# Attention's scores and values cut into more and narrower matmuls in a two-layer hybrid trunk

## Chip, cores and metric

The kernel runs on one core of one Trainium2 chip. The metric is the device time of one execution in microseconds (us); the time before is the median of three runs.

## What is computed

The reference runs two layers over 256 tokens of 2048 channels. Each layer has a convolution branch and an attention branch that read one input projection, are gated, merged and projected out. What matters here is the attention: 16 heads, queries and keys of 128 + 64 (rotary) elements, values of 128, and a mask by chunks of 64 tokens.

```python
def chunk_causal_attention(q, k, v):
    ...
        s = jnp.einsum('bqhd,bkhd->bhqk', q_i, k,
                       preferred_element_type=jnp.float32) * scale
        q_chunk = (i * Q_BLOCK + jnp.arange(Q_BLOCK)) // CHUNK
        mask = key_chunk[None, :] <= q_chunk[:, None]
        s = jnp.where(mask, s, -jnp.inf)
        p = jax.nn.softmax(s, axis=-1).astype(v.dtype)
        return jnp.einsum('bhqk,bkhd->bqhd', p, v)
    ...
    o = lax.map(block, (qb, jnp.arange(nb)))
```

Two query blocks of 128 tokens are swept. The first sees 128 keys, the second 256.

## The kernel before

**Precision.** Matmul operands are float32r. Each float32 operand is split into a high part (a copy to float32r) and a low part (the rest); a product is the sum of high x high, low x high and high x low, three matmuls into one PSUM accumulator.

**The big products.** All weights stream from HBM in 680 pieces (`raw`) of two k-tiles. ScalarE writes the high part `hi` of a piece (`split_hi`, line 211), VectorE the low part `lo` (`split_lo`, line 220), and TensorE multiplies (`product`, lines 325 to 360) into the `acc` tiles, twelve matmuls a piece, 512 columns each for most. A piece is one *slot*. The tokens are two tiles, `t` = 0 and 1.

**What sets the order.** Every engine's instructions are issued in program order (`InOrder`, lines 127 to 144; line 135 is where all of them are recorded, so all rows of the profile say L135). Between two pieces `background` (line 252) lets due steps run: `at_slot(ahead, f, vec, act)` files a step for a slot with its cost in microseconds on VectorE and ScalarE, and what those engines have left over in a slot is filled with taps of the convolution (`fill`, `run_fill`, line 281; `tap`, line 972; `assist` lets ScalarE scale a tap ahead). So a smaller cost for a step moves taps earlier.

**Attention.** It runs in pairs of heads, 8 pairs a layer, as steps between the pieces (`attention`, line 763; slots at the head of the file). For a pair, `qk_t` holds the transposed operands: `nope_t[:, 0]` and `[:, 1]` are the high and low parts of q, `[:, 2]` and `[:, 3]` those of k; `rope_t[:, 0]` is the rotary part of q (high part in one half of the partitions, low part in the other), `rope_t[:, 1]` that of k (its high part in both halves), `rope_l` the low part of k with zeros in the other half. `rope_k` is a view of `rope_t[:, 1]` and `rope_l` together.

- `scores` (line 835): the first query tile goes to `s0`, of two halves of 128 columns a head. One matmul streams two runs of 128 key columns side by side (high and low parts of k), so the halves have to be added afterwards: three matmuls a head, of 256, 128 and 256 columns. The second query tile goes to `s1`: five matmuls a head of 256 columns, straight into one accumulator.
- `maxima` (line 859): ScalarE copies one half of `s0` into `sx` in SBUF, VectorE adds the other half, masks, and takes the negated maxima of `sx` and `s1`.
- `exponentials` (line 873) on ScalarE, then the probabilities are turned and split into `pt`, high and low.
- `values` (line 899): into `o_ps`, again two halves a head: matmuls of 512, 128, 256 and 256 columns. `outputs` (line 911): ScalarE copies one half into `o_sb`, VectorE adds the other.

In the trace the PSUM tiles of the scores are named `s`, the buffers of `pt` and of the values `pv`.

Of the kernel before, what the change touches and what calls it, by code (L numbers as in the profile page):

```python
# [11 lines left out]
F32 = mybir.dt.float32  # L12
# [3 lines left out]
ALU = mybir.AluOpType  # L16
AX = mybir.AxisListType
PSUM = bass.MemoryType.PSUM

P = 128  # L20
T = 2
SEQ = 256
# [17 lines left out]
CHUNK = 64  # L40
EPS = 1e-6
MASKED = -3.0e38
# [26 lines left out]
STATS_AT, SCALE_AT, QK_BACK_AT, QK_TURN_AT, NOPE_AT, ROPE_AT, SCORES_AT = 2, 4, 7, 11, 12, 14, 17  # L69
EXP_AT, P_BACK_AT, P_TURN_AT, P_SPLIT_AT, VALUES_AT, O_AT = 19, 23, 28, 29, 32, 34  # L70
# [53 lines left out]
def trunk(ctx: ExitStack, tc: tile.TileContext, xT, x, g_in, pos, win, wuq, wukv, wpc, wpm, wo, cst, rows, invf, out):  # L124
# [19 lines left out]
    pe, vec, act, gps, sp = (InOrder(e) for e in (nc.tensor, nc.vector, nc.scalar, nc.gpsimd, nc.sync))  # L144
# [7 lines left out]
    work = pool("work", 1)  # L152
# [7 lines left out]
    tp_p = pool("tp", 1, space=PSUM)  # L160
    s_p = pool("s", 1, space=PSUM)
# [68 lines left out]
    steps, clock, late, early = [], [0], [], []  # L230
    fill, budget, marks, owed, assist = deque(), {"vec": 0.0, "act": 0.0}, {}, [], []

    def at_slot(ahead, f, vec=0.0, act=0.0, first=False):
        steps.insert(0 if first else len(steps), (clock[0] + ahead, (vec, act), f))
# [328 lines left out]
    for l in range(DEPTH):  # L563
# [84 lines left out]
        A = SimpleNamespace(pairs={}, rotary={})  # L648

        def attention_tiles(A=A, l=l):  # L650
            qk_t = big.tile([P, 16 * SEQ], F32R, tag="big", name=f"qk_t{l}")
            A.nope_t = qk_t[:, : 8 * SEQ].rearrange("p (i h s) -> p i h s", i=4, h=2)
            A.rope_t = qk_t[:, 8 * SEQ : 12 * SEQ].rearrange("p (i h s) -> p i h s", i=2, h=2)
            A.rope_k = qk_t[:, 10 * SEQ : 14 * SEQ].rearrange("p (i h s) -> p i h s", i=2, h=2)
            A.rope_l = qk_t[:, 12 * SEQ : 14 * SEQ].rearrange("p (h s) -> p h s", h=2)
            gps.memset(A.rope_l.bitcast(F32), 0.0)
            pv = big.tile([P, 4096], F32R, tag="big", name=f"pv{l}")
            A.pt = pv[:, : 2 * 768].rearrange("p (i h q) -> p i h q", i=2, h=2)
            v_parts = [pv[:, 1536 + i * 512 : 2048 + i * 512] for i in range(5)] + [qk_t[:, 14 * SEQ :]]
            v_parts = [a.rearrange("p (t h d) -> p t h d", t=T, h=2) for a in v_parts]  # L660
            A.v_split = [v_parts[2 * j : 2 * j + 2] for j in range(3)]
            A.o_sb = big.tile([P, N_HEADS, SEQ], F32, tag="big", name=f"o_sb{l}")
            A.rinv = layer_c.tile([P, T, N_HEADS], F32, tag="rinv", name="rinv")

        def pair_of(b, A=A):
            if b not in A.pairs:


                A.pairs[b] = dict(
                    qk=work2.tile([P, T, 4, 6, 32], F32, tag="qk", name="qk"),  # L670
                    vh=A.v_split[b % 3][0],
                    vl=A.v_split[b % 3][1],
                    ss=small.tile([P, 2, T, 2], F32, tag="ss_p", name="ss_p"),
                )
            return A.pairs[b]
# [86 lines left out]

        def attention(b, pair_of=pair_of, ss_d=ss_d, kpe=kpe, ccq=ccq, ssq_t=ssq_t, gqk=gqk, A=A):
            p, st = pair_of(b), {}
            nope_t, rope_t, rope_k, rope_l = A.nope_t, A.rope_t, A.rope_k, A.rope_l
            qk, ss = p["qk"], p["ss"]

            def stats():
# [64 lines left out]
                at_slot(1, lambda: [vec.tensor_sub(lo, z, hi.bitcast(F32)) for lo, z, hi in subs], 1.8)  # L833

            def scores():
                s0 = s_p.tile([P, 2, 2, P], F32, tag="s0", name="s0")
                s1 = s_p.tile([P, 2, SEQ], F32, tag="s1", name="s1")

                for h in range(2):
                    qs = slice(0, P)  # L840
                    pe.matmul(s0[:, h], rope_t[:, 0, h, qs], rope_k[:, :, h, qs], start=True, stop=False)
                    pe.matmul(s0[:, h, 0, :], nope_t[:, 1, h, qs], nope_t[:, 2, h, qs], start=False, stop=False)
                    pe.matmul(s0[:, h], nope_t[:, 0, h, qs], nope_t[:, 2:4, h, qs], start=False, stop=True)
                for h in range(2):
                    qs = slice(P, SEQ)
                    terms = [
                        (rope_t[:, 0, h, qs], rope_t[:, 1, h, :]),
                        (nope_t[:, 0, h, qs], nope_t[:, 2, h, :]),
                        (nope_t[:, 0, h, qs], nope_t[:, 3, h, :]),
                        (nope_t[:, 1, h, qs], nope_t[:, 2, h, :]),  # L850
                        (rope_t[:, 0, h, qs], rope_l[:, h, :]),
                    ]
                    for n, (qa, ka) in enumerate(terms):
                        pe.matmul(s1[:, h, :], qa, ka, start=n == 0, stop=n == len(terms) - 1)
                st["s"] = s0, s1

                late.append(maxima)

            def maxima():
                s0, s1 = st["s"]  # L860
                sx = work.tile([P, 2, P], F32, tag="sx", name="sx")
                act.copy(sx, s0[:, :, 1, :])
                vec.tensor_add(sx, s0[:, :, 0, :], sx)
                for s, nkeys in ((sx, P), (s1, SEQ)):

                    vec.memset(s[:CHUNK, :, nkeys - CHUNK :], MASKED)
                nb = small.tile([P, T, 2], F32, tag="nb", name="nb")
                vec.tensor_reduce(nb[:, 0], sx, axis=AX.X, op=ALU.max, negate=True)
                vec.tensor_reduce(nb[:, 1], s1, axis=AX.X, op=ALU.max, negate=True)
                vec.tensor_mul(nb, nb, st["rs"])  # L870
                st["s"], st["nb"] = (sx, s1), nb

            def exponentials():

# [24 lines left out]
            def values():  # L899


                st["o"] = tp_p.tile([P, 2, 2, SEQ], F32, tag="tp", name="o_ps")
                pt, v = A.pt, (p["vh"], p["vl"])
                for h in range(2):
                    o = st["o"][:, h]
                    pe.matmul(o, v[0][:, 0, h, :], pt[:, :, h, :SEQ], start=True, stop=False)
                    pe.matmul(o[:, 0, P:], v[1][:, 1, h, :], pt[:, 0, h, SEQ:], start=False, stop=False)
                    pe.matmul(o[:, :, P:], v[0][:, 1, h, :], pt[:, :, h, SEQ:], start=False, stop=False)
                    pe.matmul(o[:, 0, :], v[1][:, 0, h, :], pt[:, 0, h, :SEQ], start=False, stop=True)

            def outputs():
                o = A.o_sb[:, 2 * b : 2 * b + 2, :]
                act.copy(o, st["o"][:, :, 0, :])
                late.append(lambda: vec.tensor_add(o, st["o"][:, :, 1, :], o))
                A.pairs.pop(b)

            def later(ahead, *args, **kw):
                at_slot(ahead + PAIR_LATER[b], *args, **kw)
# [4 lines left out]
            later(QK_TURN_AT, blockwise, 1.85)  # L923
            later(NOPE_AT, split_nope, 0.0, 1.8)
            later(ROPE_AT, split_rope, 0.0, 2.5)
            later(SCORES_AT, scores, 1.85, 0.35)
            later(EXP_AT, exponentials, 0.0, 3.3)
            later(P_BACK_AT, lambda: back_in("p"))
            later(P_TURN_AT, turn_p, 0.9)
            later(P_SPLIT_AT, split_p, 0.0, 0.8)  # L930
            later(VALUES_AT, values)
            later(O_AT, outputs, 0.62, 0.6)


        us, vs, keep = {}, {}, {"separated": {}}
        s1 = layer_c.tile([P, 2, SEQ], F32, tag="s1c", name="s1c")
# [339 lines left out]
        for kind, i, pl in planned:  # L1276
            if kind == "glu":
                at = EVAC_AT
                if i == 0 and l == 0:
                    at = 6  # L1280
# [18 lines left out]
            elif kind == "uq":  # L1299
                if i == 0:  # L1300
                    attention_tiles()
# [3 lines left out]
                if block == 2:  # L1305
                    at_slot(EVAC_AT + LAST_ROTATE_AT, lambda b=GROUP * group + 3: rotate_q(b), 1.3)
                    attention(GROUP * group + 2)
# [137 lines left out]
```

## Time and profile before

| what | value |
|---|---|
| time, median of three runs | 1876.65 us (1876.35 to 1876.85) |
| span of the profiled execution, first to last instruction | 1875.0 us |
| granted TensorE clock, mean | 1.000 |
| TensorE busy, matmuls | 1869.4 us, 8577 matmuls |
| VectorE busy | 1578.0 us |
| ScalarE busy | 1360.5 us |
| GpSimd busy | 495.7 us |
| rows of matmuls into `s` / `o_ps` | 256 / 128 |

The page gives the profiled execution's span and no other time for it; the median of the runs is 1.65 us longer. In the rows, an instruction is named by line, engine, operation and out<-in tiles, then a count. PE is a matmul, PEld its weight load (LDWEIGHTS), which overlaps matmuls. Matmuls overlap each other in the pipeline, so the sum of their durations is more than the time they take; the spacing of their starts is what counts. In the list of waits a row gives who waited for whom, the sum in us, how often, and the longest. In the list of groups, the columns are count | busy us, mean ns of one | idle us before them and what ended it.

### The profile page before, as it was taken

To read this page: it belongs to the slowest core of one execution; us is meant where nothing else is said; L and a number is where in the kernel's file an instruction comes from. 1 tells how busy PE (TensorE), PEld (TensorE's weight loads), DVE (VectorE), ACT (ScalarE), POOL (GpSimd) and SP (SyncE) were. 2 spreads that over 40 slices of the span, in tenths; PEclk is the share of its full clock that TensorE was granted. 3 is DMA by queue.
4 is the path that set the end of the run, shared out by engine and by line. 5 is a ranking of instruction groups with operands and counts; after the bars stand their busy time and mean duration, and the time that the engine had idled before them with its cause. 6 is when DMAs were issued, how large, how long until landed. Compare 5 with 4: busy or idle time off the path is not lost.

```text
span 1875.0 us, 27166 instructions
## 1 busy us (share of the span) xinstructions
PE 1869.4 (100%) x8577; PEld 1570.9 (84%) x8577; DVE 1578.0 (84%) x2453; ACT 1360.5 (73%) x2510; POOL 495.7 (26%) x942
## 2 busy tenths in 40 slices
PE   9999999999999999999999999999999999999999
PEld 8988888888888888888899888888888888888887
DVE  6899998898999988766679899889899999885664
ACT  7678888888888876644557688788889888574442
POOL 1055555542200000122221455555322000001210
PEclk9999999999999999999999999999999999999999
DMA  9688878787765566678876787887877556667775
GB/s 322 219 264 255 261 256 258 257 275 226 244 204 192 194 207 218 208 239 278 290 234 216 260 267 253 260 255 262 267 231 242 196 191 204 206 206 222 239 250 166
DMA packets 138960, 445.05 MB, mean 237 GB/s; under 512 B 23680, under 2 KB 29312, under 8 KB 138816
## 3 DMA queue, kind: packets, MB, share of 16 engines
q1 hardware_dynamic: 105120, 359.89, 59.2%
q0 software_dynamic: 32832, 82.62, 13.8%
q8 instruction: 67, 1.10, 0.2%
q10 hardware_dynamic: 864, 0.80, 0.1%
q14 instruction: 77, 0.63, 0.1%
HBM read 399.18 MB, written 44.04 MB: 236 GB/s over the span
## 4 chain that ended last, share of the span: by engine, by line
PE 99%; DMA 1%; DVE 0%; ACT 0%; SPq 0%; issue 0%; DVEq 0%
PE acc L135 96%; PE s L135 2%; PE o_ps L135 1%; DMA raw<-in_win 0%; DMA gx<-in_g 0%; DVE xres L135 0%; ACT hi L135 0%; PE var L135 0%; PE mu L135 0%; SPq L135 0%; DVEq L135 0%
## 5 line engine op out<-in xcount | busy, mean ns | idle before, releaser
L135 ACT CAST hi<-raw 128x1024 fp32r<-128x1024 f32 (+3 forms) x682 | 700.3, 1033 | 405.0 <-PE acc L135 348.9
L135 DVE TENSOR_TENSOR lo<-raw,hi 128x1024 fp32r<-128x1024 f32 (+3 forms) x682 | 814.0, 1195 | 191.5 <-PE acc L135 145.7
L135 PE MATMUL acc<-hi,hT 128*128 128x512 f32 (+2 forms) x1728 | 419.6, 382 | 0.0
L135 PEld LDWEIGHTS acc<-hi,hT 128*128 128x128 f32 x1728 | 319.6, 188 | 59.1
L135 PE MATMUL acc<-hi,h_hi 128*128 128x512 f32 (+2 forms) x864 | 260.5, 383 | 1.3 <-ACT hi L135 1.3
L135 PE MATMUL acc<-hi,h_lo 128*128 128x512 f32 (+2 forms) x864 | 260.1, 382 | 0.0
L135 ACT ACTIVATE tap<-u_t,cst 128x256 f32<-128x256 f32 x542 | 235.7, 501 | 2.8 <-DVE v_t L135 2.8
L135 PE MATMUL acc<-lo,h_hi 128*128 128x512 f32 (+2 forms) x864 | 229.7, 382 | 0.0
L135 PE MATMUL acc<-lo,hT 128*128 128x512 f32 (+2 forms) x864 | 229.3, 382 | 0.0
L135 DVE TENSOR_TENSOR v_t<-v_t,tap 128x512 f32<-128x512 f32 x271 | 186.4, 688 | 9.7 <-DVE v_t L135 0.9
L135 POOL DMA_DIRECT2D turned<-turn_d x88 | 49.4, 562 | 531.0 <-DVE v_t L135 315.0
L135 PEld LDWEIGHTS acc<-hi,h_lo 128*128 128x128 f32 x864 | 161.0, 188 | 30.1
L135 PEld LDWEIGHTS acc<-hi,h_hi 128*128 128x128 f32 x864 | 160.0, 188 | 30.9 <-ACT hi L135 2.2
L135 PEld LDWEIGHTS acc<-lo,h_hi 128*128 128x128 f32 x864 | 160.5, 188 | 30.2 <-DVE lo L135 0.3
L135 PEld LDWEIGHTS acc<-lo,hT 128*128 128x128 f32 x864 | 160.6, 188 | 29.9
L135 DVE SCALAR_TENSOR_TENSOR v_t<-u_t,cst,v_t 128x256 f32<-128x256 f32 x418 | 178.4, 480 | 2.0
L135 POOL DMA_DIRECT2D turn_d<-gate x184 | 100.5, 554 | 290.6 <-DVE gate L135 177.6
L135 PE MATMUL acc<-hi,ycT 128*128 128x512 f32 x512 | 127.8, 389 | 0.0
L135 PE MATMUL acc<-hi,oT 128*128 128x512 f32 x512 | 127.7, 389 | 0.0
L135 PE MATMUL acc<-hi,yT 128*128 128x512 f32 x512 | 127.5, 388 | 0.0
L135 PE MATMUL acc<-hi,qkc 128*128 128x512 f32 x448 | 115.4, 389 | 0.0
L135 PEld LDWEIGHTS acc<-hi,ycT 128*128 128x128 f32 x512 | 96.1, 188 | 20.0
(176 smaller groups left out, 2227.1 us busy)
## 6 DMA issues: line engine op xcount, KB each, us to landing
raw<-in_win SPq DMA_DIRECT2D x382, 512.0 KB, 4.2
raw<-in_wpm SPq DMA_DIRECT2D x64, 512.0 KB, 3.3
raw<-in_wpc SPq DMA_DIRECT2D x64, 512.0 KB, 4.2
raw<-in_wo SPq DMA_DIRECT2D x64, 512.0 KB, 4.9
raw<-in_wukv SPq DMA_DIRECT2D x32, 512.0 KB, 4.1
turned<-turn_d POOLq DMA_DIRECT2D x56, 256.0 KB, 4.7
raw<-in_win SPq DMA_DIRECT2D x32, 384.0 KB, 4.6
raw<-in_wuq SPq DMA_DIRECT2D x24, 512.0 KB, 4.3
```

The source lines that it names most:

```text
L135: ins = getattr(self.engine, name)(*a, **k)
```

## The change

For the first query tile `scores` now issues the same five products a head as for the second, each over one run of 128 key columns and all into one accumulator `s0` of 128 columns a head. `maxima` masks and reduces both PSUM tiles directly; `sx`, its copy and its addition go, and the exponentials read `s0` in PSUM. `values` issues six products a head, three of 256 columns (first key tile) and three of 128 (second key tile, seen by the second query tile alone), all into one accumulator; `outputs` is one copy. The planner's costs of the two steps are lowered: scores from 1.85 and 0.35 us to 1.4 and 0.0 (VectorE, ScalarE), outputs from 0.62 to 0.0 on VectorE.

```diff
@@ attention_tiles
-            A.rope_k = qk_t[:, 10 * SEQ : 14 * SEQ].rearrange("p (i h s) -> p i h s", i=2, h=2)
@@ scores
-                s0 = s_p.tile([P, 2, 2, P], F32, tag="s0", name="s0")
-                s1 = s_p.tile([P, 2, SEQ], F32, tag="s1", name="s1")
-
-                for h in range(2):
-                    qs = slice(0, P)
-                    pe.matmul(s0[:, h], rope_t[:, 0, h, qs], rope_k[:, :, h, qs], start=True, stop=False)
-                    pe.matmul(s0[:, h, 0, :], nope_t[:, 1, h, qs], nope_t[:, 2, h, qs], start=False, stop=False)
-                    pe.matmul(s0[:, h], nope_t[:, 0, h, qs], nope_t[:, 2:4, h, qs], start=False, stop=True)
-                for h in range(2):
-                    qs = slice(P, SEQ)
-                    terms = [
...
-                    for n, (qa, ka) in enumerate(terms):
-                        pe.matmul(s1[:, h, :], qa, ka, start=n == 0, stop=n == len(terms) - 1)
-                st["s"] = s0, s1
+                st["s"] = tuple(s_p.tile([P, 2, (t + 1) * P], F32, tag=f"s{t}", name=f"s{t}") for t in range(T))
+
+                for t, s in enumerate(st["s"]):
+                    qs, keys = slice(t * P, (t + 1) * P), slice(0, (t + 1) * P)
+                    for h in range(2):
+                        terms = [
+                            (rope_t[:, 0, h, qs], rope_t[:, 1, h, keys]),
+                            (nope_t[:, 0, h, qs], nope_t[:, 2, h, keys]),
+                            (nope_t[:, 0, h, qs], nope_t[:, 3, h, keys]),
+                            (nope_t[:, 1, h, qs], nope_t[:, 2, h, keys]),
+                            (rope_t[:, 0, h, qs], rope_l[:, h, keys]),
+                        ]
+                        for n, (qa, ka) in enumerate(terms):
+                            pe.matmul(s[:, h, :], qa, ka, start=n == 0, stop=n == len(terms) - 1)
@@ maxima
-                s0, s1 = st["s"]
-                sx = work.tile([P, 2, P], F32, tag="sx", name="sx")
-                act.copy(sx, s0[:, :, 1, :])
-                vec.tensor_add(sx, s0[:, :, 0, :], sx)
-                for s, nkeys in ((sx, P), (s1, SEQ)):
-
-                    vec.memset(s[:CHUNK, :, nkeys - CHUNK :], MASKED)
                 nb = small.tile([P, T, 2], F32, tag="nb", name="nb")
-                vec.tensor_reduce(nb[:, 0], sx, axis=AX.X, op=ALU.max, negate=True)
-                vec.tensor_reduce(nb[:, 1], s1, axis=AX.X, op=ALU.max, negate=True)
+                for t, s in enumerate(st["s"]):
+                    vec.memset(s[:CHUNK, :, (t + 1) * P - CHUNK :], MASKED)
+                    vec.tensor_reduce(nb[:, t], s, axis=AX.X, op=ALU.max, negate=True)
                 vec.tensor_mul(nb, nb, st["rs"])
@@ values
-                st["o"] = tp_p.tile([P, 2, 2, SEQ], F32, tag="tp", name="o_ps")
+                st["o"] = tp_p.tile([P, 2, SEQ], F32, tag="tp", name="o_ps")
                 pt, v = A.pt, (p["vh"], p["vl"])
                 for h in range(2):
-                    o = st["o"][:, h]
-                    pe.matmul(o, v[0][:, 0, h, :], pt[:, :, h, :SEQ], start=True, stop=False)
-                    pe.matmul(o[:, 0, P:], v[1][:, 1, h, :], pt[:, 0, h, SEQ:], start=False, stop=False)
-                    pe.matmul(o[:, :, P:], v[0][:, 1, h, :], pt[:, :, h, SEQ:], start=False, stop=False)
-                    pe.matmul(o[:, 0, :], v[1][:, 0, h, :], pt[:, 0, h, :SEQ], start=False, stop=True)
+                    for t, own, at in ((0, slice(0, SEQ), slice(0, SEQ)), (1, slice(P, SEQ), slice(SEQ, SEQ + P))):
+                        for vi, pi in ((0, 0), (0, 1), (1, 0)):
+                            pe.matmul(
+                                st["o"][:, h, own], v[vi][:, t, h, :], pt[:, pi, h, at],
+                                start=(t, vi, pi) == (0, 0, 0), stop=(t, vi, pi) == (1, 1, 0),
+                            )
@@ outputs
-                o = A.o_sb[:, 2 * b : 2 * b + 2, :]
-                act.copy(o, st["o"][:, :, 0, :])
-                late.append(lambda: vec.tensor_add(o, st["o"][:, :, 1, :], o))
+                act.copy(A.o_sb[:, 2 * b : 2 * b + 2, :], st["o"])
@@
-            later(SCORES_AT, scores, 1.85, 0.35)
+            later(SCORES_AT, scores, 1.4, 0.0)
-            later(O_AT, outputs, 0.62, 0.6)
+            later(O_AT, outputs, 0.0, 0.6)
```

In the built order TensorE's rows change only inside these groups. At the first pair's scores of the first layer, between matmuls of the running big product (`acc`), as one piece of the difference (`s_2073` is `s0`, `s_2074` is `s1`):

```order
 L135 MATMUL acc_0_1909<-lo_1990,h_hi 128x512 x2
 L135 MATMUL acc_1_1910<-lo_1990,h_hi 128x512 x2
-L135 MATMUL s_2073<-qk_t_1397 128x256
-L135 MATMUL s_2073<-qk_t_1397 128x128
-L135 MATMUL s_2073<-qk_t_1397 128x256 x2
-L135 MATMUL s_2073<-qk_t_1397 128x128
-L135 MATMUL s_2073<-qk_t_1397 128x256
+L135 MATMUL s_2073<-qk_t_1397 128x128 x10
 L135 MATMUL s_2074<-qk_t_1397 128x256 x10
 L135 MATMUL acc_0_1909<-hi_1992,h_hi 128x512 x2
```

Six matmuls into `s0` become ten of 128 columns; the ten into `s1` and the neighbours stay.

TensorE at the first pair's values, before:

```order
L135 MATMUL acc_1_2311<-lo_2499,h_hi 128x512 x2
L135 MATMUL o_ps<-pv_1399 128x512
L135 MATMUL o_ps<-pv_1399 128x128
L135 MATMUL o_ps<-pv_1399 128x2x128
L135 MATMUL o_ps<-pv_1399 128x256
L135 MATMUL o_ps<-pv_1399 128x512
L135 MATMUL o_ps<-pv_1399 128x128
L135 MATMUL o_ps<-pv_1399 128x2x128
L135 MATMUL o_ps<-pv_1399 128x256
L135 MATMUL acc_0_2593<-hi_2501,qkc_155 128x512 x4
```

and now:

```order
L135 MATMUL acc_1_2312<-lo_2506,h_hi 128x512 x2
L135 MATMUL o_ps<-pv_1399 128x256 x3
L135 MATMUL o_ps<-pv_1399 128x128 x3
L135 MATMUL o_ps<-pv_1399 128x256 x3
L135 MATMUL o_ps<-pv_1399 128x128 x3
L135 MATMUL acc_0_2603<-hi_2508,qkc_155 128x512 x4
```

Eight matmuls have become twelve, in the same place.

VectorE after the first pair's scores (`maxima`, then low parts of weights and taps `v_t`), before:

```order
L135 TENSOR_TENSOR sx<-s_2073,sx 128x256
L135 MEMSET sx 64x2x64
L135 MEMSET s_2074 64x2x64
L135 TENSOR_REDUCE nb<-sx 128x2
L135 TENSOR_REDUCE nb<-s_2074 128x2
L135 TENSOR_TENSOR nb<-nb,r_p 128x4
L135 TENSOR_TENSOR lo_2102<-raw_1915,hi_2057 128x1024
L135 SCALAR_TENSOR_TENSOR v_t<-u_t,cst,v_t 128x256 x2
L135 TENSOR_TENSOR lo_2130<-raw_1951,hi_2104 128x1024
```

and now:

```order
L135 MEMSET s_2073 64x2x64
L135 TENSOR_REDUCE nb<-s_2073 128x2
L135 MEMSET s_2074 64x2x64
L135 TENSOR_REDUCE nb<-s_2074 128x2
L135 TENSOR_TENSOR nb<-nb,r_p 128x4
L135 TENSOR_TENSOR lo_2103<-raw_1915,hi_2057 128x1024
L135 SCALAR_TENSOR_TENSOR v_t<-u_t,cst,v_t 128x256 x4
L135 TENSOR_TENSOR lo_2133<-raw_1951,hi_2105 128x1024
```

The addition is gone, and two instructions of a tap that stood later have moved up ahead of the next low part. The orders of SyncE and GpSimd, which issue the DMAs, are the same as before.

More of the change, by code (lines that the diff above doesn't have):

```diff
@@ L764, in attention @@
             p, st = pair_of(b), {}
-            nope_t, rope_t, rope_k, rope_l = A.nope_t, A.rope_t, A.rope_k, A.rope_l
+            nope_t, rope_t, rope_l = A.nope_t, A.rope_t, A.rope_l
             qk, ss = p["qk"], p["ss"]
@@ L844, in scores @@
-                for h in range(2):
-                    qs = slice(P, SEQ)
-                    terms = [
[L847 to L852, printed above, removed]
-                    for n, (qa, ka) in enumerate(terms):
-                        pe.matmul(s1[:, h, :], qa, ka, start=n == 0, stop=n == len(terms) - 1)
@@ L869, in maxima @@
-                vec.tensor_reduce(nb[:, 1], s1, axis=AX.X, op=ALU.max, negate=True)
+                for t, s in enumerate(st["s"]):
+                    vec.memset(s[:CHUNK, :, (t + 1) * P - CHUNK :], MASKED)
+                    vec.tensor_reduce(nb[:, t], s, axis=AX.X, op=ALU.max, negate=True)
                 vec.tensor_mul(nb, nb, st["rs"])
-                st["s"], st["nb"] = (sx, s1), nb
+                st["nb"] = nb
             def exponentials():
```

## The prediction

> **What bounds the kernel now.** I read the page first: the busy shares and the chain of work that ended last.
>
> ```profile
> span 1875.0 us, 27166 instructions
> ...
> PE 1869.4 (100%) x8577; PEld 1570.9 (84%) x8577; DVE 1578.0 (84%) x2453; ACT 1360.5 (73%) x2510; POOL 495.7 (26%) x942
> ...
> PEclk9999999999999999999999999999999999999999
> ...
> PE 99%; DMA 1%; DVE 0%; ACT 0%; SPq 0%; issue 0%; DVEq 0%
> PE acc L135 96%; PE s L135 2%; PE o_ps L135 1%; DMA raw<-in_win 0%; DMA gx<-in_g 0%; DVE xres L135 0%; ACT hi L135 0%; PE var L135 0%; PE mu L135 0%; SPq L135 0%; DVEq L135 0%
> ```
>
> The chain is TensorE for 99%, and what the change rewrites stands on it: `s` (scores) 2%, `o_ps` (values) 1%. The granted clock is 0.9 or more in every slice. A busy TensorE is not proof of one that never waits, since ends of matmuls are modelled; so I asked next for the waits of the matmul and weight-load rows, and then for the longest pieces of the chain in order of time (start, length, what).
>
> ```profile
> PE acc L135 <- ACT hi L135: 1.3, 2, 0.9
> PE warm L135 <- PEq L1434: 0.8, 1, 0.8
> ...
> PEld acc L135 <- ACT hi L135: 2.2, 3, 1.4
> PEld warm L135 <- issue: 0.8, 1, 0.8
> PEld acc L135 <- DVE lo L135: 0.3, 1, 0.3
> ```
>
> ```profile
> 12.19 164.67 PE acc L135 x804
> 178.74 32.67 PE acc L135 x144
> ...
> 294.11 24.50 PE acc L135 x108
> 329.84 24.50 PE acc L135 x108
> ```
>
> All that TensorE waited is 1.3 + 0.8 us before matmuls and 2.2 + 0.8 + 0.3 us before weight loads, and the pieces of the chain show it running without a break from 12.19 us on. The second piece gives a price: 144 matmuls of 512 columns in 32.67 us are 0.227 us each, from start to start. The two engines that feed it are ahead of it, as the list of waits of all engines says:
>
> ```profile
> ACT hi L135 <- PE acc L135: 348.9, 277, 2.6
> DVE lo L135 <- PE acc L135: 145.7, 112, 1.8
> ```
>
> ScalarE's high parts and VectorE's low parts of the weights wait for matmuls to give their buffers back, not the other way round. So the time is a sum of matmul spacings plus the start and the tail, and only what changes that sum counts.
>
> **TensorE's part of the change.** The columns streamed do not change. Scores of the first query tile before, per head: 256 + 128 + 256 = 640; after: five products of 128 = 640. Values before, per head: 512 + 128 + 256 + 256 = 1152; after: 3 x 256 + 3 x 128 = 1152. What changes is into how many matmuls they are cut: 6 become 10 in the scores, 8 become 12 in the values, and each brings a weight load of its own. So the price of a 128-column matmul decides. The durations of the rows do not give it, since they overlap; starts do. TensorE's timeline over one pair's scores (start, length from the first start to the last end, count), then the same list from narrower windows, where a row that groups matmuls begins with the first still open:
>
> ```profile
> 176.69 2.05 PE L135 MATMUL s<-qk_t 128*128 128x256 f32 x16
> 178.58 0.40 PE L135 MATMUL acc<-hi,h_hi 128*128 128x512 f32 x1
> ...
> 177.38 0.40 PE L135 MATMUL s<-qk_t 128*128 128x256 f32 x2
> ...
> 176.81 0.40 PE L135 MATMUL s<-qk_t 128*128 128x128 f32 x2
> ...
> 176.87 0.45 PE L135 MATMUL s<-qk_t 128*128 128x256 f32 x2
> ```
>
> The sixteen matmuls take 178.58 - 176.69 = 1.89 us. The last ten, of 256 columns, run from 177.38 to 178.58: **0.120 us** each. The first six, four of 256 columns and two of 128, take 0.69 us; less 4 x 0.120 that leaves 0.21, or 0.105 us for one of 128. But the recorded starts put only 176.87 - 176.81 = 0.06 us between a 128-column matmul and the next one. The weight-load rows at the same place settle how I read that:
>
> ```profile
> 176.81 0.19 PEld L135 LDWEIGHTS s<-qk_t 128*128 128x128 f32 x1
> ...
> 176.92 0.19 PEld L135 LDWEIGHTS s<-qk_t 128*128 128x128 f32 x1
> ...
> 177.04 0.19 PEld L135 LDWEIGHTS s<-qk_t 128*128 128x128 f32 x1
> ```
>
> Loads begin 0.11 and 0.12 us apart even across the 128-column matmul: a load holds its place for about 0.11 us, the short matmul ends in half of that, and the next one, though recorded as begun, waits for its weights. The values give the same price a second time:
>
> ```profile
> 221.32 1.32 PE L135 MATMUL o_ps<-pv 128*128 128x512 f32 x8
> 222.47 0.39 PE L135 MATMUL acc<-hi,qkc 128*128 128x512 f32 x1
> ```
>
> Eight matmuls in 222.47 - 221.32 = 1.15 us: two of 512 columns (2 x 0.227), four of 256 (4 x 0.120), and 0.216 left for two of 128, 0.108 each. Bounds for a row of ten of them, which no trace shows: from below 0.105 (the scores), from above 0.120, the spacing of ten loads in a row where each carries 256 columns. Further down lies only the recorded 0.06, a rival. I take **0.108**, the weight-load gap and the values agreeing on it.
>
> - Scores of a pair: 10 x 0.108 + 10 x 0.120 = 2.28 us, before 1.89: +0.39.
> - Values of a pair: 6 x 0.120 + 6 x 0.108 = 1.37 us, before 1.15: +0.22.
> - Pairs: 8 a layer, two layers, 16. 16 x 0.61 = **+9.7 us**. With 0.105 it is 16 x (0.36 + 0.20) = +9.0, with 0.120 it is 16 x (0.51 + 0.29) = +12.8.
>
> That the halves are no longer strided side by side I price at nothing: with strided products priced like the others (0.120 in the scores, 0.227 in the values) the two groups leave 0.105 and 0.108 for a short matmul, so a stride can hardly cost more than that difference.
>
> **What VectorE and ScalarE are relieved of.** The groups of their instructions, by form:
>
> ```profile
> L135 DVE TENSOR_TENSOR o_sb<-o_ps,o_sb 128x512 f32<-128x512 f32 x16 | 11.0, 687 | 2.7 <-ACT o_sb L135 2.7
> L135 DVE TENSOR_REDUCE nb<-s 128x2 f32<-128x512 f32 x16 | 10.7, 667 | 0.0
> L135 DVE TENSOR_TENSOR sx<-s,sx 128x256 f32<-128x256 f32 x16 | 6.8, 425 | 27.4 <-ACT sx L135 27.4
> L135 DVE TENSOR_REDUCE nb<-sx 128x2 f32<-128x256 f32 x16 | 5.6, 353 | 0.0
> ...
> L135 ACT COPY sx<-s 128x256 f32<-128x256 f32 x16 | 6.0, 373 | 18.3 <-PE s L135 18.3
> ```
>
> Per pair VectorE loses the two additions, 0.687 + 0.425 = 1.11 us, and ScalarE the copy of 0.373 us. Reading the first tile's scores out of PSUM in place of `sx` I take as free: the maximum over 512 PSUM elements costs 0.667, twice the 0.353 over 256 in SBUF within 6%. All of it, 17.8 us on VectorE and 6.0 us on ScalarE, and the 27.4 us for which VectorE stood waiting for the copy, lies beside a TensorE that waits for neither: worth 0 to the end. The planner is told of it, 0.45 + 0.62 = 1.07 us a pair less for VectorE and 0.35 for ScalarE, and spends it on convolution taps, so they stand earlier, not that the engine idles. SyncE's and GpSimd's orders do not change, nor does any DMA. No wait is added: `s0` is now held until the exponentials have read it, as `s1` was already, and the next pair's scores come 329.84 - 294.11 = 35.7 us later (the last two pieces of the chain above, each between a pair's values and the next pair's scores).
>
> **Sum.** The profiled span is 1875.0 us, 1.65 below the median 1876.65 of the runs; I add the change to both. Span 1884.7, time 1876.65 + 9.7 = **1886.4 us**. What a measurement of this kernel can tell from no change is about 0.2%, 3.8 us: it ends at 1872.9 and 1880.4.
>
> **Rivals.**
>
> 1. *The recorded 0.06 is the true spacing* of short matmuls in a row, the load being drawn far enough ahead. Then scores cost 0.60 + 1.20 - 1.89 = -0.09, values 0.72 + 0.36 - 1.15 = -0.07 a pair, 16 x -0.16 = -2.6: 1874.1, not slower than before. Place: the ten 128-column matmuls of each pair. It decides from 10p + 1.20 - 1.89 + 0.72 + 6p - 1.15 = 0, a spacing p of 0.070. For it speaks the matmul rows' starts; against it that both groups then come out 0.09 to 0.10 us longer than their parts. Chance 4%.
> 2. *Loads overlap one another in a long row of short matmuls.* A load's row is 0.19 long while loads begin 0.11 apart, so there is overlap already, and ten alike might halve the gap between 0.06 and 0.108: p = 0.084 gives 16 x (0.15 + 0.07) = +3.6, 1880.2. Against it: the one gap between loads that a short matmul spans is 0.11, not less. Chance 5%. [...]
> 3. *Load and matmul take turns* where there is nothing long to hide the load: p = 0.108 + 0.06 = 0.168, scores +0.99, values +0.58, 16 x 1.57 = +25.1: 1901.8. Against it: the 0.21 and 0.216 us left for two short matmuls hold one load each and no more. Chance 4%. [...]
> 4. *TensorE begins to wait for a low part.* The planner puts earlier taps between VectorE's subtractions; two instructions more ahead of a `lo` (row below) delay it by 2 x 0.480 = 0.96 us.
>
> ```profile
> L135 DVE SCALAR_TENSOR_TENSOR v_t<-u_t,cst,v_t 128x256 f32<-128x256 f32 x418 | 178.4, 480 | 2.0
> ```
>
>    Queued behind it on VectorE are the next `lo` and the evacuations. Once in each pair would be 16 x 0.96 = 15.4 on top, 1901.8; two or three times is 1888 to 1889. Against it: VectorE is given as many microseconds as it is told to fill, and it waited 145.7 us for TensorE where TensorE waited 0.3 for it. Chance 7%.
>
> That the change does not do what it says can be left out: the built order shows the ten short matmuls a pair.
>
> **How the numbers follow.** Forecast 80%, rivals 4, 5, 4 and 7%. The forecast by its bounds is 1876.65 + 9.0 = 1885.7 to 1876.65 + 12.8 = 1889.5. The range is **1884.9 to 1890.5**: the forecast's, with 0.8 us below for rounding in rows read to 0.01 us, and 1.0 above for the mild form of rival 4. It leaves out rivals 1, 2, 3 and part of 4. Faster by over 0.2%: 0.01, the rest of rival 1 lying within the bound. Within 0.2%: 0.08 (rivals 1 and 2). Slower: 0.91.
>
> **What would show it.** In the profile after: 320 rows of score matmuls (16 x 20, where 16 x 16 = 256 stood) and 192 of the values (16 x 12); from the start of a pair's first score matmul to the next `acc` 2.28 us, of the values 1.37; weight loads 0.11 apart in the run of ten. 2.88 and 1.73 would be rival 3's turns, 1.80 and 1.08 rival 1. A row of TensorE waiting for `lo` of more than a microsecond would be rival 4, and gaps between `acc` matmuls with it. A granted clock below 1 in any slice, or spacings other than 0.227 for 512 columns, would take the ground from under the sum.

## The result, and the profile after

The changed kernel takes **1886.24 us** (five runs, 1885.83 to 1887.04) against 1876.65 (five, 1875.73 to 1876.85): a ratio of 1.0053, 95% interval 1.0041 to 1.0066. It is slower by 9.6 us, where 9.7 were forecast. The span of its profiled execution went from 1875.0 to 1884.3 us, 9.3 more.

The page after, in the lines that answer to those of before: busy times, clock, and the chain.

```profile
span 1884.3 us, 27334 instructions
...
PE 1880.1 (100%) x8705; PEld 1583.1 (84%) x8705; DVE 1570.7 (83%) x2436; ACT 1341.8 (71%) x2464; POOL 494.1 (26%) x942
...
PEclk9999999999999999999999999999999999999999
...
PE 100%; DVE 0%; issue 0%; DVEq 0%
```

128 matmuls and 128 weight loads have come (8577 to 8705; 320 rows into `s` and 192 into `o_ps`). VectorE and ScalarE are busy for 7.3 and 18.7 us less, not for the 17.8 and 6.0 us that the change takes off them. ScalarE's further 13.0 us are 30 scalings of taps that it no longer does (its row before and after, below). VectorE does these taps alone now: 448 rows of `v_t<-u_t,cst,v_t` where 418 stood, for 15 additions of scaled taps fewer. That is a part of why its busy time fell by less.

```profile
L135 ACT ACTIVATE tap<-u_t,cst 128x256 f32<-128x256 f32 x542 | 235.7, 501 | 2.8 <-DVE v_t L135 2.8
```

```profile
L135 ACT ACTIVATE tap<-u_t,cst 128x256 f32<-128x256 f32 x512 | 222.7, 499 | 3.2 <-DVE v_t L135 2.8
```

The chain is still TensorE alone. Did TensorE wait for anything new? Its waits, matmuls and then loads, and the two large waits of its feeders:

```profile
PE warm L135 <- PEq L1420: 0.8, 1, 0.8
```

```profile
PEld warm L135 <- issue: 0.8, 1, 0.8
PEld acc L135 <- ACT hi L135: 0.6, 2, 0.3
```

```profile
ACT hi L135 <- PE acc L135: 394.7, 293, 4.4
...
DVE lo L135 <- PE acc L135: 160.3, 123, 1.8
```

No. The feeders are further ahead than before (394.7 us of waiting against 348.9, 160.3 against 145.7). The time is in the matmuls that were re-cut. TensorE's timeline over the first pair's scores and over its values:

```profile
176.04 2.46 PE L135 MATMUL s<-qk_t 128*128 128x128 f32 x20
178.34 0.40 PE L135 MATMUL acc<-hi,h_hi 128*128 128x512 f32 x1
...
221.49 1.49 PE L135 MATMUL o_ps<-pv 128*128 128x256 f32 x12
222.82 0.44 PE L135 MATMUL acc<-hi,qkc 128*128 128x512 f32 x1
...
222.82 0.68 PE L135 MATMUL acc<-hi,qkc 128*128 128x512 f32 x2
```

The scores take 178.34 - 176.04 = 2.30 us (1.89 before, 2.28 forecast), the values 222.82 - 221.49 = 1.33 (1.15 before). The values seem 0.04 cheaper than the 1.37 forecast, but the 0.44 behind the last row gives them away: I read it as the `acc` matmul recorded at 222.82 waiting for a load that the short matmul ahead could not hide, since one of 512 columns lasts 0.39 otherwise. A pair's whole cost is best read from the chain, from the end of one pair's values to the end of the next one's:

```profile
295.70 24.55 PE acc L135 x108
332.06 24.55 PE acc L135 x108
```

36.36 us from pair to pair where 329.84 - 294.11 = 35.73 stood: +0.63 a pair, and 16 x 0.63 = 10.1. The span grew by 9.3, 0.8 less, and 0.65 of that lies ahead of any changed matmul: the first scores start at 176.04 in this execution and at 176.69 in the one before. The waits for the first weights differ (1.3 us before matmuls in the profile before, none after). It looks like scatter between executions: in the profiles of the experiments below the first scores start at 175.57 in `half_weights` and at 176.31 in `wide_scores`.

Inside the run of ten, the weight loads from narrow windows of the timeline, each row beginning with the first load still open:

```profile
176.04 0.30 PEld L135 LDWEIGHTS s<-qk_t 128*128 128x128 f32 x2
...
176.15 0.30 PEld L135 LDWEIGHTS s<-qk_t 128*128 128x128 f32 x2
...
176.26 0.30 PEld L135 LDWEIGHTS s<-qk_t 128*128 128x128 f32 x2
...
176.37 0.30 PEld L135 LDWEIGHTS s<-qk_t 128*128 128x128 f32 x2
```

They start 0.11 us apart, one after the other, as the single short matmuls of before had suggested.

### The profile page after: what moved, and what is told of

It reads as the page before. It is cut to its first block, busy times and chain, and to the rows that moved or that the text cites. A ratio compares the mean times of both kernels' runs of the same rounds, so it can differ in the third digit from the quotient of the medians.

```text
span 1884.3 us, 27334 instructions
## 1 busy us (share of the span) xinstructions
PE 1880.1 (100%) x8705; PEld 1583.1 (84%) x8705; DVE 1570.7 (83%) x2436; ACT 1341.8 (71%) x2464; POOL 494.1 (26%) x942
## 3 DMA queue, kind: packets, MB, share of 16 engines
q8 instruction: 68, 1.11, 0.2%
## 4 chain that ended last, share of the span: by engine, by line
PE 100%; DVE 0%; issue 0%; DVEq 0%
PE acc L135 96%; PE s L135 2%; PE o_ps L135 1%; PE warm L135 0%; DVE xres L135 0%; PE var L135 0%; PE mu L135 0%; DVEq L135 0%
## 5 line engine op out<-in xcount | busy, mean ns | idle before, releaser
L135 ACT CAST hi<-raw 128x1024 fp32r<-128x1024 f32 (+3 forms) x682 | 699.9, 1032 | 459.5 <-PE acc L135 394.7
L135 DVE TENSOR_TENSOR lo<-raw,hi 128x1024 fp32r<-128x1024 f32 (+3 forms) x682 | 813.9, 1195 | 219.1 <-PE acc L135 160.3
L135 ACT ACTIVATE tap<-u_t,cst 128x256 f32<-128x256 f32 x512 | 222.7, 499 | 3.2 <-DVE v_t L135 2.8
L135 DVE SCALAR_TENSOR_TENSOR v_t<-u_t,cst,v_t 128x256 f32<-128x256 f32 x448 | 191.1, 478 | 2.1
L135 DVE TENSOR_TENSOR v_t<-v_t,tap 128x512 f32<-128x512 f32 x256 | 175.8, 687 | 8.2
```

The source lines that it names most:

```text
L135: ins = getattr(self.engine, name)(*a, **k)
```

## The experiments

The theory: a matmul of 128 columns is held to about 0.11 us by the load of the next 128 weight columns, so the change costs TensorE 0.63 us a pair, and nothing that it gives VectorE and ScalarE reaches the end. Rivals: replanned taps make TensorE wait; narrow products stream slowly, or wait for one another in the accumulator; every added matmul costs a fixed share. Each experiment has its own runs of the kernel before on the same chip (medians of 1875.8 to 1876.3 us). The edits are shown in part, with `...` where lines are left out.

### One half of the change at a time

`scores_only` takes the changed `scores` and `maxima` and puts back the values:

```diff
...
-                st["o"] = tp_p.tile([P, 2, SEQ], F32, tag="tp", name="o_ps")
+                st["o"] = tp_p.tile([P, 2, 2, SEQ], F32, tag="tp", name="o_ps")
...
-            later(O_AT, outputs, 0.0, 0.6)
+            later(O_AT, outputs, 0.62, 0.6)
```

> The changed scores and maxima, with the values and outputs of before. Theory (a 128-column matmul is held to 0.11 us by the weight load behind it): the scores' part of the sum alone, 16 x 0.39 to 0.41 = 6.2 to 6.6 us over before, 1882.9 to 1883.3. Rival (the loss is a wait of the feeding engines, caused by the replanned taps): no fixed share; near 1876.7 or near 1886.2, with TensorE rows that wait.

Measured 1882.84 us, ratio 1.0036 (1.0023 to 1.0048), +6.8 over its own before of 1876.07. `values_only` is the reverse, the changed `values` and `outputs` in the kernel before.

> The changed values and outputs, with the scores and maxima of before. Theory: 16 x 0.22 = 3.5 us over before, 1880.2; together with scores_only the two add up to the whole change. Rival (replanned taps): the two do not add up.

Measured 1879.26, ratio 1.0017 (1.0008 to 1.0025), +3.2. The two add up to 10.0, the change measured 9.6. The chain's pieces agree; first `scores_only`, then `values_only`:

```profile
331.36 24.50 PE acc L135 x108
367.51 24.50 PE acc L135 x108
```

```profile
330.11 24.55 PE acc L135 x108
366.06 24.55 PE acc L135 x108
```

36.15 and 35.95 from pair to pair, +0.42 and +0.22 over 35.73. A loss from replanned taps would have no reason to split like that, and in neither profile does TensorE wait for more than 1.4 us for any one feeder.

### The relief alone

```diff
...
-                act.copy(sx, s0[:, :, 1, :])
-                vec.tensor_add(sx, s0[:, :, 0, :], sx)
+                sx = s0[:, :, 0, :]
...
-                late.append(lambda: vec.tensor_add(o, st["o"][:, :, 1, :], o))
+            later(SCORES_AT, scores, 1.4, 0.0)
+            later(O_AT, outputs, 0.0, 0.6)
```

> TensorE's matmuls of before, but the second halves of the first tile's scores and of the values are left out of the sums: no copy into sx, no addition of it, one copy of the values without the addition, and the planner's costs of the change. Theory: VectorE's 17.8 us and ScalarE's 6.0 us lie beside TensorE, 1876.65 within 0.7. Rival (they hold TensorE up somewhere): up to 17 us faster; a gain of 2 us or more would show it, and the change's own loss would then be larger than it looks.

Measured 1876.12 against 1876.07, ratio 1.0 (0.9991 to 1.0009). VectorE and ScalarE are as busy as in the changed kernel (1571.1 and 1341.2 us, there 1570.7 and 1341.8), so the whole relief is in it. What the change takes off the two engines is worth nothing to the end of this kernel.

### More short matmuls

`second_tile_cut` also cuts the second query tile's scores:

```diff
-                            pe.matmul(s[:, h, :], qa, ka, start=n == 0, stop=n == len(terms) - 1)
+                            for c in range(t + 1):
+                                own = slice(c * P, (c + 1) * P)
+                                pe.matmul(
+                                    s[:, h, own], qa, ka[:, own],
+                                    start=n == 0 and c == 0, stop=n == len(terms) - 1 and c == t,
+                                )
```

> The changed kernel with the second query tile's scores cut too, 20 matmuls of 128 columns a pair in place of 10 of 256; the same columns. Theory: 20 x 0.111 - 10 x 0.120 = 1.02 us a pair, 16.3 us over the changed kernel, 1902.5. Rival (a fixed cost for every added matmul, 9.6 us / 128 = 0.075): 160 x 0.075 = 12.0 over it, 1898.2. Rival (loads hidden better in a longer run): less than 10 over it.

Measured 1903.07, ratio 1.0143 (1.0128 to 1.0159) to before, 16.8 over the changed kernel: the theory's 16.3, not the 12.0 of a fixed cost. Its timeline at the first pair's scores:

```profile
176.07 3.46 PE L135 MATMUL s<-qk_t 128*128 128x128 f32 x30
179.37 0.44 PE L135 MATMUL acc<-hi,h_hi 128*128 128x512 f32 x1
```

Thirty short matmuls in 3.30 us: 0.110 each, over a run three times as long.

### Load or stream: half the columns, half the weights

Both rivals left give 0.11 for a 128-column product too: slow streaming, and waits in the accumulator. `half_columns` halves the stream and keeps the loads. To leave half the keys out it masks them for all 128 queries of the first tile; the reference masks them for the first 64 alone:

```diff
-                    qs, keys = slice(t * P, (t + 1) * P), slice(0, (t + 1) * P)
+                    qs, keys = slice(t * P, (t + 1) * P), slice(0, SEQ if t else CHUNK)
...
-                    vec.memset(s[:CHUNK, :, (t + 1) * P - CHUNK :], MASKED)
+                    vec.memset(s[: CHUNK if t else P, :, (t + 1) * P - CHUNK :], MASKED)
```

> The changed kernel, but the first query tile's scores are taken for the first 64 keys alone (the other 64 are masked for every query): ten matmuls of 64 columns a pair in place of ten of 128, with the same weight loads. Theory (the load of 128 weight columns sets the spacing): the spacing in the run stays at 0.11 and the time at 1886.2 within 0.7. Rival (a narrow product streams at about half speed, 0.11 for 128 columns): spacing about 0.055, 16 x 10 x 0.055 = 8.8 less, 1877.4.

`half_weights` halves the loads and keeps the stream:

```diff
-                    qs, keys = slice(t * P, (t + 1) * P), slice(0, (t + 1) * P)
+                    qs, keys = slice(t * P, SEQ if t else CHUNK), slice(0, (t + 1) * P)
...
```

> The changed kernel, but the first query tile's scores are taken for the first 64 queries alone (the others are set to zero): ten weight loads of 64 columns a pair in place of 128, with the same 128 columns streamed. Theory: the load halves to about 0.055 and 128 columns at full rate remain, about 0.067; 16 x 10 x 0.044 = 7.0 less than the changed kernel, 1879.2. Rival (narrow products stream slowly, or wait for one another in the same accumulator): spacing stays at 0.11, 1886.2.

The scores of a pair in `half_columns`, then in `half_weights` (the columns name weights, rows by columns, and the product's output):

```profile
175.85 2.46 PE L135 MATMUL s<-qk_t 128*128 128x64 f32 x20
178.15 0.40 PE L135 MATMUL acc<-hi,h_hi 128*128 128x512 f32 x1
```

```profile
175.57 2.01 PE L135 MATMUL s<-qk_t 128*64 128x128 f32 x20
177.41 0.40 PE L135 MATMUL acc<-hi,h_hi 128*128 128x512 f32 x1
```

Half the columns change nothing: 2.30 us, and 1886.12 against the changed kernel's 1886.24. Half the weights give 1.84 us, 0.46 less over ten matmuls, so about 0.065 each, and 1878.93, 7.3 us less where 7.0 were expected (7.2 less than `half_columns`, which ran on the same chip). The loads follow, 0.11 apart in the first and 0.06 in the second:

```profile
175.97 0.30 PEld L135 LDWEIGHTS s<-qk_t 128*128 128x128 f32 x2
176.08 0.30 PEld L135 LDWEIGHTS s<-qk_t 128*128 128x128 f32 x2
```

```profile
175.57 0.20 PEld L135 LDWEIGHTS s<-qk_t 128*64 128x64 f32 x2
175.63 0.19 PEld L135 LDWEIGHTS s<-qk_t 128*64 128x64 f32 x2
```

The same 128 columns into the same accumulator, one behind the other, run at 0.065 when the load is short. That settles it for the load, with one reserve: the rows of the output are halved with the columns of the weights, and no run parts the two. The load of 128 columns shows as 0.11 us between loads; what one of 64 takes alone no run shows, since 128 columns are streamed behind each and the spacing is 0.065.

### The opposite edit

If narrow costs, wide should save a little. `second_tile_wide` goes back to the kernel before and lays the second tile's scores side by side as well:

```diff
...
-                        pe.matmul(s1[:, h, :], qa, ka, start=n == 0, stop=n == len(terms) - 1)
+                    pe.matmul(s1[:, h], rope_t[:, 0, h, qs], rope_k[:, :, h, :], start=True, stop=False)
+                    pe.matmul(s1[:, h, 0, :], nope_t[:, 1, h, qs], nope_t[:, 2, h, :], start=False, stop=False)
+                    pe.matmul(s1[:, h], nope_t[:, 0, h, qs], nope_t[:, 2:4, h, :], start=False, stop=True)
...
+                vec.tensor_add(sy, s1[:, :, 0, :], sy)
...
-            later(VALUES_AT, values)
+            later(VALUES_AT, lambda: values(0))
+            later(VALUES_AT + 1, lambda: outputs(0), 0.45, 0.4)
+            later(VALUES_AT + 2, lambda: values(1))
+            later(VALUES_AT + 3, lambda: outputs(1), 0.45, 0.4)
```

> The kernel before with the opposite edit: the second query tile's scores in halves side by side too (512, 256 and 512 columns a head in place of five of 256), one copy and one addition more, and the values taken a head at a time to free a PSUM bank. Theory (a matmul of n columns costs n columns and a small fixed share): 2 x 0.120 become 0.227 four times a pair, 16 x 4 x 0.013 = 0.8 us less than before, 1875.8, if ScalarE and VectorE, with 2 us a pair more to do, still keep ahead. Rival (they do not): TensorE rows that wait, and a time over 1876.65.

Measured 1905.52, ratio 1.0159 (1.0145 to 1.0173). `second_tile_wide_b` moved the values up a slot:

```diff
...
+            later(VALUES_AT - 1, lambda: values(0))
+            later(VALUES_AT, lambda: outputs(0), 0.45, 0.4)
...
```

> second_tile_wide with the values of the two heads each a slot earlier, so that the second head's values no longer come after their buffers are filled again. Theory (its 28 us were waits: TensorE for the first head's values to leave PSUM, and later for ycT): the waits for o_sb stay, 10 to 14 us, and those for ycT too if VectorE's added work is their cause; 1895 to 1906. Rival (they came from the late place of the values): near 1876.

Measured 1909.32, ratio 1.0175 (1.0159 to 1.0190). In these two, with the heads taken one at a time, the attention's values are not the reference's. The reason that the second expectation names is not the cause, which stays open, so the two say what waits, and no more. TensorE's loads waited in the first:

```profile
PEld o_ps L135 <- DVE o_sb L135: 14.3, 10, 2.4
PEld acc L135 <- ACT ycT L135: 10.6, 3, 5.0
```

The first row is the one buffer of `o_ps`, which the values of the two heads now use in turn: the loads wait 14.3 us for VectorE's additions out of it. The second was new to me: `ycT`, the split output of the convolution branch, comes late; I suspected that VectorE had more to do than it had room for. `burden_alone` asks that by itself, on the kernel before with its matmuls untouched:

```diff
...
+                act.activation(sy, s1, AF.Copy, scale=0.5)
                 vec.tensor_add(sx, s0[:, :, 0, :], sx)
+                vec.scalar_tensor_tensor(sy, s1, 0.5, sy, op0=ALU.mult, op1=ALU.add)
...
-            later(SCORES_AT, scores, 1.85, 0.35)
+            later(SCORES_AT, scores, 2.5, 0.95)
```

> The kernel before, TensorE's matmuls as they were, with more work on the other side: the second tile's scores are copied by ScalarE and added by VectorE at half weight each (0.69 us more for VectorE and about 0.6 for ScalarE a pair, and planned so). Theory (the cover at the end of the convolution is wide: the first split of ycT ends at 750 us and is first used at 765): 8 x 0.7 = 5.6 us a layer fit into 15, no change, 1876.1 within 1. Rival (that cover is already used up, as the waits for ycT in second_tile_wide suggest): TensorE waits for ycT, 5 us or more slower.

Measured 1889.66, ratio 1.0074 (1.0061 to 1.0086): the rival, and my reading of the cover was wrong. ScalarE's splits of `ycT` in the first layer, in the kernel before, in the changed one and in this one (start, length, two casts a row):

```profile
748.81 1.15 ACT L135 CAST ycT<-v_t 128x512 fp32r<-128x512 f32 x2
758.70 1.14 ACT L135 CAST ycT<-v_t 128x512 fp32r<-128x512 f32 x2
768.30 1.14 ACT L135 CAST ycT<-v_t 128x512 fp32r<-128x512 f32 x2
774.91 1.15 ACT L135 CAST ycT<-v_t 128x512 fp32r<-128x512 f32 x2 [1.41 <-DVE v_t L135]
```

```profile
739.72 1.13 ACT L135 CAST ycT<-v_t 128x512 fp32r<-128x512 f32 x2
...
766.92 1.14 ACT L135 CAST ycT<-v_t 128x512 fp32r<-128x512 f32 x2
```

```profile
759.15 1.13 ACT L135 CAST ycT<-v_t 128x512 fp32r<-128x512 f32 x2
...
791.92 1.14 ACT L135 CAST ycT<-v_t 128x512 fp32r<-128x512 f32 x2 [3.68 <-DVE v_t L135]
```

I had judged by the first cast, 15 us before its use at 765.0. The later casts decide. A piece takes 12 x 0.227 = 2.72 us, and the last two of the eight pieces on `ycT` are due from 765.0 + 6 x 2.72 = 781.3; before, the first cast of the last row ended near 775.5, less than 6 us ahead. In this run that row starts 17 us later. That is more than the additions alone come to (eight pairs at 0.69 us, 5.5 us); the run also plans for them, and it does not part the work from the plan. In the changed kernel the row starts 8.0 us earlier while its use moves some 4 us later (first `ycT` matmul at 769.3): there the relief went into a reserve that nothing draws on.

`wide_scores` then takes the same wide scores with the changed kernel's values, so that VectorE's load stays level. Against the kernel before:

```diff
...
+                vec.tensor_add(sy, s1[:, :, 0, :], sy)
...
-                late.append(lambda: vec.tensor_add(o, st["o"][:, :, 1, :], o))
...
```

> The wide scores of second_tile_wide (512, 256 and 512 columns a head for the second query tile) with the values of the changed kernel: VectorE gains the addition of the halves, 0.69 us a pair, and loses that of the values, 0.69, so that nothing is piled on it. Theory (a matmul of n columns costs n columns and a small share of its own, and the waits of second_tile_wide and burden_alone were those of an overfull VectorE): a pair's scores take 1.85 us in place of 1.89, the time is that of values_only less 16 x 0.04 = 0.6, 1878.6, and TensorE has no rows that wait for ycT. Rival (the waits come with the wide scores themselves): TensorE waits for ycT again, 1885 or more.

```profile
176.31 2.01 PE L135 MATMUL s<-qk_t 128*128 128x256 f32 x12
178.16 0.63 PE L135 MATMUL acc<-hi,h_hi 128*128 128x512 f32 x2
```

```profile
PEld acc L135 <- ACT hi L135: 1.1, 2, 0.9
PEld warm L135 <- issue: 0.8, 1, 0.8
```

Scores of a pair 1.85 us, no wait for `ycT`, and 1878.97 us, ratio 1.0015 (1.0006 to 1.0024). ScalarE's added copy is that of `burden_alone` (0.587 us a pair, there 0.598) and the scores are planned at the same cost; only VectorE's load is level. So the late `ycT` there points to VectorE's additions and their plan, and not to ScalarE's copies. The last row of casts is close even here:

```profile
779.27 1.15 ACT L135 CAST ycT<-v_t 128x512 fp32r<-128x512 f32 x2 [2.03 <-DVE v_t L135]
```

Its first cast ends near 779.9, and the piece that needs it starts at 782.34. Next to `values_only` (1879.26) the 0.3 less is within the measurement; that the wide scores save 0.04 a pair is seen in the trace alone. None of the kernels beats the one before.

## Why the prediction was right

- *What bounds it.* TensorE's spacings alone: right. Its waits after are 0.8 us before matmuls and 1.4 before loads, and `relief_alone` measured no difference for the relief of the other engines. Only the size of that relief was off: ScalarE's was 18.7 us and not 6.0, since 30 tap scalings moved from it to VectorE, and VectorE's 7.3 and not 17.8. It costs the sum nothing.
- *The price of a short matmul.* 0.108 taken, 0.110 measured over thirty in a row. That it is the load was read from the gaps between loads; `half_columns` (2.30 us for a pair's scores) and `half_weights` (1.84) show it. The recorded start, 0.06 us after a short matmul's, is not when the next one runs (rival 1, which asked for 1874.1).
- *Scores* +0.39 a pair forecast, +0.41 to 0.42 measured; *values* +0.22 and 0.22; 16 x 0.61 = 9.7 against 10.1 from the chain and 9.6 between the medians. That the medians came within 0.1 of the forecast is luck: the chain and the two halves of the change (10.0 together) say that it was 0.3 to 0.4 short. The scatter of the kernel before hides that (its median was 1876.65 here and 1875.8 to 1876.3 in the experiments). The start-up, which I had not considered, is a part of it: 0.65 us between the two profiled executions.
- *VectorE's maxima out of PSUM taken as free.* They are on no path, so the sum holds, but the reason was loose: in the changed kernel the maximum over 256 elements takes 0.424 us on average in PSUM, where it took 0.353 from `sx`.
- *Rivals 2 and 3*, loads that overlap more or take turns: they asked for 0.084 and 0.168, and the 0.110 over thirty in a row excludes both. *Rival 4*: TensorE did not wait for a low part once.
- What the prediction did not see: the feeders' lead that it read from their waits is that of the weights' parts; at `ycT` it was less than 6 us. The forecast did not need it, since the change takes work off. Taking 1.11 us a pair off VectorE gained nothing; putting 0.69 us a pair on it, with 0.6 on ScalarE, cost 13.5 us.

## What to carry to other kernels

When TensorE is the bound, count matmuls by the larger of their stream and their weight load, not by columns alone: with float32r weights of 128 columns a matmul cost 0.11 us here whether 64 or 128 columns were streamed, 0.120 with 256 and 0.227 with 512 (widths between 128 and 256 were not measured), and with weights of 64 columns 0.065 for 128 streamed. So one product of 256 columns cut in two cost 0.22 in place of 0.120, while one of 512 cut in two would come to 0.240 in place of 0.227. Read the price from the gaps between weight loads or from the length of a whole group, not from a short matmul's recorded start or duration (0.06 us to the next start in the profile before, 0.270 long on average in the one after, where the price was 0.110). And an engine from which work can be taken for nothing (`relief_alone`, 0 us) may still have no room for more (`burden_alone`, 13.5 us lost): look at the last of its deliveries, not the first.

## What was not expected of the hardware

After TensorE had waited 4.60 us for `ycT` in `burden_alone`, its matmuls ran slowly for a while. Its loads with the wait, then matmuls, then the granted clock by stretches, the last of them inside the slow matmuls (the columns are busy time and count of the five engines, PEclk, DMA share, GB/s):

```profile
780.45 0.30 PEld L135 LDWEIGHTS acc<-hi,ycT 128*128 128x128 f32 x2 [4.60 <-ACT ycT L135]
```

```profile
782.63 1.48 PE L135 MATMUL acc<-hi,ycT 128*128 128x512 f32 x3
783.91 1.38 PE L135 MATMUL acc<-lo,ycT 128*128 128x512 f32 x4
```

```profile
700.00:770.00 70.00, 70.00 (x313) 58.02 (x311) 56.73 (x82) 45.22 (x60) 3.28 (x6) 1.00 0.66 218
...
780.00:800.00 20.00, 14.97 (x45) 11.38 (x46) 9.02 (x13) 5.21 (x7) 0.00 (x0) 0.74 0.19 66
```

```profile
781.20:784.30 3.10, 3.10 (x7) 2.47 (x8) 0.53 (x1) 0.11 (x1) 0.00 (x0) 0.50 0.01 5
```

Three matmuls of 512 columns from 782.63 to 783.91 are 0.427 us each in place of 0.227. The granted clock is 0.74 over the 20 us with the waits and 0.50 in two stretches, from about 781.2 to 784.3 and from about 791.4 to 798.3. The first begins 0.7 us after the matmuls had started again. The second begins before the second wait, of 5.00 us, ends at 792.59.

TensorE's loads waited twice for those casts, 9.6 us together (its matmuls 8.8), and the kernel lost 13.5. An estimate of the rest: it multiplied for 3.1 and 5.7 us at half the clock, which loses half of that, 4.4, and 8.8 + 4.4 = 13.2. What brings the clock down no run shows; the trace shows it at 0.50 behind a wait of 4.60 us and around the end of one of 5.00.
